# Six key pages of the attention stage summed in branch A, and two adaLN pieces and q's last transposes later, in a hybrid decoder layer on one core

## The chip, the core and the metric

The kernel runs on one core of one Trainium2 chip. A core has five engines with a queue of instructions each: TensorE (PE in the profile, its weight loads PEld), VectorE (DVE), ScalarE (ACT), GpSimd (POOL) and SyncE (SP), which issues most of the transfers and computes nothing. Transfers can be issued on SP's, ACT's or POOL's queue; 16 DMA engines carry them all. The metric is the device time of one execution in microseconds (us); lower is better.

## The reference

One layer of a decoder runs for two groups that share the weights: a prompt of 512 tokens and 8 samples of one token each, 520 columns in all, with a width of 1024.

```python
sh1, sc1, g1, sh2, sc2, g2 = ada_modulation(c, ada_w, ada_b)     # silu(c) @ ada_w + ada_b, six rows
h = rms_norm(x, norm1_g) * (1.0 + sc1) + sh1
z = h @ w_in                        # -> xr, gr, q, k, v, forget logits fl, ga, gb
xc, conv_new = causal_dwconv(xr, conv_buf, conv_w, conv_b)
hr, h_last = rg_lru(xc, h0, ...)    # recurrent branch
ya = (hr * gelu(gr)) @ w_proj_a                                  # branch A
logf = log_sigmoid(fl + b_f)
yb = attend(q, k, v, logf) @ w_proj_b                            # branch B
x = x + g1 * ((sigmoid(ga) * ya + sigmoid(gb) * yb) @ w_o)
h2 = rms_norm(x, norm2_g) * (1.0 + sc2) + sh2
gu, up = split(h2 @ w_ffn_in, 2)
x = x + g2 * ((silu(gu) * up) @ w_ffn_out)                       # then a last RMSNorm
```

The prompt's `attend` is causal attention in blocks, with 16 heads of width 64. Each of the samples attends to 1024 past tokens, which lie in a cache as 8 pages of 128 tokens; a page table says which:

```python
k_all = concatenate([cache_k[page_table], k]); v_all = concatenate([cache_v[page_table], v])
s = einsum(q, k_all) * scale + Fk[query] - Fk[key]               # Fk: cumulative log forget
out = einsum(softmax(s), v_all)
```

So there are 8 x 8 = 64 key pages and as many value pages, each 128 tokens x 1024 numbers, 512 KB.

## The kernel before, in words

**Units.** Everything is held transposed, 128 rows of the width to a tile with all 520 columns. A weight matrix is taken in *units* of 128 output columns. A unit is one product: for each of two halves of the columns, 8 blocks of the inner width times 3 passes (high and low parts of weights and activations), 24 matmuls a half. `begin` (line numbers are those of the profile) opens each unit: it calls `tick` for units 0 to 41, loads weights ahead (`load_chunks`, line 186, on SP's queue, two raw buffers `wraw`), splits them into a high and a low part (`split_upto`: ACT writes `whi`, line 210, DVE writes `wlo`, line 211; three buffers each), and flushes stores. The matmuls of a unit are line 245, and the profile names them by what they write: `xr`, `gr`, `ga`, `gb`, `k`, `v`, `pa`, `pb`, `fig`, `fiu`, `fo`.

**Order.** q comes first (q6 and q7 are units 0 and 1). Then the recurrent branch in four pairs i = 0, 2, 4, 6: `conv` (product xr, then the convolution on DVE, line 893, and a split into `xch`, `xcl`), `gelu` (product gr), `gate_a` and `gate_b` (products ga, gb), `lru_gates` (small products), `lru_exp`, `lru_root`, `lru_scan`, `lru_mul`, `lru_g` (which splits `g`, line 279). For i = 0 the units are 2 to 7, for i = 2 units 8 to 15, for i = 4 units 16 to 23, for i = 6 units 24 to 31. Unit 32 is k0; units 33 to 39 and 41 are branch A (`branch_a`, product pa, eight of them), with v0 as unit 40. `decay_rows(0)` after k0 prepares the masks of two heads on POOL (lines 1113 and 1115).

Then the attention steps i = 0 to 7 follow, one for two heads each: product k(i+1), with `v_tokens` in its middle, `turn` (transposes of the probabilities to `ptt`, split into `ph` and `pl`, line 1160), product v(i+1), with `turn` and the first `scores` in its middle, `values` (matmuls `po`), the rest of `scores`. `scores` leaves half the scaling of the probabilities to POOL (line 1146). After them come the output product of branch B (pb), the merge (wo), and the FFN (fig, fiu, fo), which takes more than a third of the time.

**Key pages.** The samples' scores are computed on DVE. For each page `page_load` reads its number from the table and issues the load (line 622), into one of seven buffers `pg`; `key_sums` multiplies it by the sample's q, copied to all partitions (`qb`; line 667, or line 663 for half pages), and sums over each head (line 668 or 664) into `S`. `key_pages` takes the next entries of a list of 64, of which the first 16 are pairs of half pages of samples 0 and 1. `tick` calls both: sums for entries that were loaded two ticks ago (one tick for the first units), then `KEYS[n]` new loads for unit n, and in the attention steps the four calls of `at(i, 0..3)` with `KEYS_AT`. When both samples of a pair r are complete, a chain of softmax steps (`past_softmax`: lines 704, 706, then `lgt`, `lgm`, `lgs` on TensorE) starts, one step every second tick. `VALUES` and `VALUES_AT` say at which ticks a pair of value pages is multiplied on TensorE (`pv`, line 751); the next pair is loaded as soon as one is used. Before, POOL's queue takes key and value loads up to the count in `LAST_LRU`, that is units 0 to 31, and SP's queue all later ones. The buffers `pg` are shared by key pages, value pages, `qb` of samples 2 to 7, and the adaLN weights.

**adaLN pieces.** Shift and scale of the first norm are made at the start (`first_mod`). The next two rows (gate1 and shift2) are `which` = 1: eight pieces of 128 rows of `ada_w`; `ada_load` loads two buffers `araw` on SP's queue (line 296), `ada_piece` runs 8 matmuls (line 308) into one PSUM bank, `ada_copy` copies it out, `ada_end` transposes it and adds the bias on DVE (line 324). PSUM has eight banks, and every half product takes one.

**q's last rows.** `q_done` copies the samples' columns of a finished q tile, stores it, and transposes the samples' columns on TensorE (line 796, `qt`); with the fourth tile `q_samples` scales and stores them to `qtd`, from where `qb` is loaded.

The order of instructions on each queue follows the program, with a planner that may let an instruction pass one that it holds not to be ready; `tc.issue_after` and `in_place` bind single ones.

Of the kernel before, what the change touches and what calls it, by code (L numbers as in the profile page):

```python
# [64 lines left out]
def kernel(ctx, tc, xT, par, gates, b_f, cst, cse, own, cache_k, cache_v, cache_lf, pt,  # L65
# [3 lines left out]
    pe, act, dve, pool, sp = nc.tensor, nc.scalar, nc.vector, nc.gpsimd, nc.sync  # L69
# [90 lines left out]
    state = {"n": 0, "dma": 0, "split": 0, "load": 22, "lead": 11, "due": 0, "age": 1}  # L160
# [8 lines left out]
    def flush():  # L169
        while stores:  # L170
# [1 line left out]

    later = {}

    KEYS = dict(zip(range(42), (2, 2, 2, 0, 3, 3, 3, 2, 1, 1, 1, 1, 2, 2, 2, 1, 0, 1, 0, 1, 2, 2, 2, 2, 0, 1, 1, 1, 2, 2, 1, 2,
                                1, 1, 1, 1, 1, 1, 1, 1, 0, 0)))
    VALUES = (19, 21, 23, 25, 27, 29, 31, 35, 37, 39)
    LAST_LRU = 32

    def load_chunks(upto):  # L180
        while state["dma"] < len(chunks) and state["dma"] <= upto:
# [76 lines left out]
    def product(name, a, evac, mid=None):  # L258
        n = begin()
        for j in range(2):  # L260
            b = bank(f"{name}_{j}")
            half_product(n, j, a, b)
            evac(j, b[:, :HALF])
            if j == 0 and mid is not None:
                mid()
        run_later(n)
# [23 lines left out]
    def ada_load(which, kq):  # L290
        if kq >= KT:
            return
        for g2 in range(2):
            raw = pgp.tile([128, 2, 512], F32, name="araw", tag="pg")
            c0 = which * 2048 + g2 * 1024
            sp.dma_start(raw, ada_w[kq * 128:kq * 128 + 128, c0:c0 + 1024].rearrange("p (g c) -> p g c", g=2))
            ada_raw.setdefault((which, kq), []).append(raw)

    def ada_piece(which, kq):
        if kq == 0:  # L300
            ada_acc[which] = bank(f"ada{which}")
        acc = ada_acc[which]
        if (which, kq) not in ada_raw:
            ada_load(which, kq)
        for g2, raw in enumerate(ada_raw.pop((which, kq))):
            for gg in range(2):
                g = 2 * g2 + gg
                pe.matmul(acc[32 * g:32 * g + 32, :], lhsT=silc[:, kq], rhs=raw[:, gg],
                          start=kq == 0, stop=kq == KT - 1, tile_position=(0, 32 * g))

    def ada_copy(which):
        sb = slot("adas", 512)
        act.copy(sb, ada_acc[which])
        ada_acc[which] = sb
# [80 lines left out]
    def past_sums(b):  # L395
        lk, after = lks[b]
        sf = bank(f"suf{b}")
        pe.matmul(sf, lhsT=cs[:, C_TRI:C_TRI + 128], rhs=lk, start=True, stop=False)
        pe.matmul(sf, lhsT=ones, rhs=after, start=False, stop=True)
        t = slot("suf", 512)  # L400
        act.copy(t, sf)
        suf.append(t)


    h = []
# [68 lines left out]
    for f in range(KT):  # L474
        t = slot("sq1")
# [14 lines left out]
    for f in range(KT):  # L490
        t = slot("xn")
# [48 lines left out]
    qtd = drp.tile([NS, D], F32, name="qtd")  # L540
# [73 lines left out]
    def page_load(cache, s, j, pg=None, c0=0, c1=D):  # L614
        if pg is None:
            pg = pgp.tile([128, D], F32, name="pg", tag="pg")
        n = s * NPAGE + j
        eng = pool if state["n"] <= LAST_LRU else sp
        done = loads[eng]
        with tc.issue_after(done[-4].ins) if len(done) >= 4 else nullcontext():  # L620
            r = eng.value_load(ptb[0:1, n:n + 1], min_val=0, max_val=NPOOL - 1)
        done.append(eng.dma_start(pg, cache[bass.ds(r, 1), :, c0:c1].rearrange("a p c -> (a p) c")))  # L622
        return pg
# [19 lines left out]
    def key_page(s, j, half=None):  # L643
        if half is not None:
            return key_halves(s, j, half)
        if j == 0:
            t = pgp.tile([128, D], F32, name="qb", tag="pg")
            (pool if state["n"] <= LAST_LRU else sp).dma_start(t, qtd[s:s + 1, :].partition_broadcast(128))
            qb[0] = t
        pg = page_load(cache_k, s, j)  # L650
        pend.append([0, s, j, pg, qb[0], None])
# [141 lines left out]
    def q_done(i, t):  # L793
        pool.tensor_copy(q8[:, NS * i:NS * i + NS], t[:, NP:])
        sp.dma_start(qd[i], t)
        pe.transpose(qtp[i // 4][:, 128 * (i % 4):128 * (i % 4) + 128], t[:, NP:], ident)
        if i % 4 == 3:
            q_samples(i // 4)
# [30 lines left out]
    for i in range(KT):  # L829
        if i % 4 == 0:  # L830
            qtp.append(bank(f"qt{i}", NS))
        if i < 6:
            t = qpart[i]
            for j, (t0, t1) in enumerate(HALVES):
                b = bank(f"q{i}_{j}")
                for k in range(4):
                    q_matmuls(1, i, j, k, b)
                dve.tensor_tensor(t[:, t0:t1], b[:, :HALF], t[:, t0:t1], ALU.add)
        else:
            t = slot("q")  # L840
            product(f"q{i}", h, to(t, act.copy))
        if ready:
            q_done(*ready.pop())
        ready.append((i, t))
        if i == 3:
            split_upto(0)
        if i == 3:
            for n in range(KT):
                gate_load(n)
        if i >= 4:  # L850
            for n in (2 * i - 8, 2 * i - 7):
                gate_split(n)
        if i == 4:
            past_load()
            split_upto(1)
            close = forget_logits()
        if i == 6:
            close()
            with tc.issue_after(state["last"].ins), tc.issue_after(state["act"].ins):
                decay()  # L860
                past_conv()
            past_turn(0)
        if i == 7:
            past_turn(1)
        if i >= 2:
            ada_piece(1, i - 2)
            ada_load(1, i - 1)
        if i == 3:
            q_done(*ready.pop())
        if i == 5:  # L870
            tick(2, 0)
    q_last = ready.pop()
# [5 lines left out]
    g = [None] * KT  # L878
    lru = {}

    def conv(i, mid=None):
        xr, xc = slot("xr"), slot("xc")

        def evac(j, b):
            t0, t1 = HALVES[j]
            act.copy(xr[:, t0:t1], b)
            act.activation(xc[:, t0:t1], b, AF.Identity, scale=cw[3], bias=prm[:, i, P_CB:P_CB + 1])

        cw = [prm[:, i, P_CW + n:P_CW + n + 1] for n in range(4)]
        product(f"xr{i}", h, evac, mid)  # L890
        for n in range(3):
            d = 3 - n
            dve.scalar_tensor_tensor(xc[:, d:NP], xr[:, :NP - d], cw[n], xc[:, d:NP], ALU.mult, ALU.add)
        dve.tensor_tensor(xc[:, NP:], xc[:, NP:], conv_past[:, i], ALU.add)
        act.copy(conv_tail[:, i], xr[:, NP - 3:])
        lru[i] = {"xc": xc}

        def close():
            lru[i].update(xs=split("xc", xc), gw=gws.pop(i))

        defer(0, close)
# [55 lines left out]
    def both(fn, i):  # L957
        fn(i)
        fn(i + 1)
# [17 lines left out]
        store(tAd[i], tA[i])  # L977

    for i in range(0, KT, 2):
        conv(i, None if i else lambda: q_done(*q_last))  # L980
        if i == 0:
            ada_piece(1, 6)
            ada_load(1, 7)
        else:
            both(lru_root, i - 2)
            gelu(i - 2)
            lru_scan(i - 2)
        conv(i + 1)
        if i == 0:
            ada_piece(1, 7)  # L990
            ada_copy(1)
        else:
            gelu(i - 1)
            lru_scan(i - 1)
            both(lru_mul, i - 2)
            both(lru_g, i - 2)
        if i < 6:
            gate_a(i)
            lru_gates(i)
            if i == 0:  # L1000
                ada_end(1)
            gate_a(i + 1)
            lru_gates(i + 1)
            gate_b(i)
            if i == 0:
                past_sums(0)
            gate_b(i + 1)
            if i == 0:
                past_sums(1)
            both(lru_exp, i)  # L1010
            if i == 2:
                log_forget()
            if i == 4:
                sum_forget()
        else:
            lru_gates(i)
            gate_a(i)
            lru_gates(i + 1)
            gate_a(i + 1)
            both(lru_exp, i)  # L1020
            gelu(i)
            both(lru_root, i)
            gelu(i + 1)
            both(lru_scan, i)
            both(lru_mul, i)
            both(lru_g, i)
# [233 lines left out]
            q_load(1)  # L1260
    g = None
    state.update(load=14, lead=8)
    KEYS_AT = [(0, 2, 0, 0)] * 3 + [(0, 0, 0, 0)] * 5
    VALUES_AT = [(1, 1, 0, 1)] * 6 + [(1, 1, 0, 1), (1, 0, 0, 0)]

    def at(i, part):
        tick(KEYS_AT[i][part], VALUES_AT[i][part])
        flush()

    for i in range(KT):  # L1270
# [313 lines left out]
```

## Time and profile before

| | us |
|---|---|
| three runs, median (lowest to highest) | 1081.26 (1080.08 to 1083.93) |
| the profiled execution | 1082.19 |
| its span, first to last instruction | 1080.5 |
| TensorE busy | 1029.1 |
| VectorE busy | 663.9 |
| ScalarE busy | 494.4 |
| GpSimd busy | 192.2 |

The profile is of one execution; times in it count from the span's start. In its rows L245 is a line of the kernel, `out<-in` names the tiles, 128x1024 is partitions by elements, x48 a count; what follows `<-` in brackets is what ended an engine's idle time before the row. "Granted clock" is the share of TensorE's full clock that it was given. `whi`, `wlo` and the like are named without their numbers, so which unit a split belongs to is counted from the order.

### The profile page before, as it was taken

How to read it: one execution, taken by the hardware profiler on the slowest of the kernel's cores; microseconds unless marked ns; L12 is line 12 of the kernel's file. 1: busy time of each engine (PE TensorE's matmuls, PEld its weight loads, DVE VectorE, ACT ScalarE, POOL GpSimd, SP SyncE). 2: the span in 40 equal slices, each digit the busy share in tenths (PEclk: the TensorE clock that was granted, in tenths of full speed). 3: DMA queues.
4: the chain of work that ended last, by engine and by line, in shares of the span. 5: the costliest groups of instructions: out<-in, count | busy, mean ns of one | idle time of the engine just before them, and what ended most of it. 6: DMA issues, size and time to landing. Idle time of an engine off the chain costs nothing.

```text
span 1080.5 us, 21007 instructions
## 1 busy us (share of the span) xinstructions
PE 1029.1 (95%) x8210; PEld 951.7 (88%) x8210; DVE 663.9 (61%) x1166; ACT 494.4 (46%) x976; POOL 192.2 (18%) x328
## 2 busy tenths in 40 slices
PE   4999899999999988899999999999999999999994
PEld 2887699999999977688888979999999999999994
DVE  5437899989989766766656546843343333433363
ACT  4423565856772455577784224533212233113251
POOL 0224320112132223433420003300000000000013
PEclk9999899999999998899999999999999999999998
DMA  9799976878879979877874764124224233233112
GB/s 329 270 316 325 302 253 175 260 258 295 253 257 292 300 251 267 263 227 239 246 247 165 262 241 108 41 78 117 79 82 115 79 88 109 79 94 103 59 59 80
DMA packets 165285, 206.95 MB, mean 192 GB/s; under 512 B 9778, under 2 KB 126018, under 8 KB 165122
## 3 DMA queue, kind: packets, MB, share of 16 engines
q1 hardware_dynamic: 150626, 160.39, 47.8%
q0 software_dynamic: 10880, 38.80, 10.6%
q10 hardware_dynamic: 3680, 6.42, 1.6%
q8 instruction: 64, 1.05, 0.4%
q14 instruction: 35, 0.29, 0.1%
HBM read 192.49 MB, written 13.09 MB: 190 GB/s over the span
## 4 chain that ended last, share of the span: by engine, by line
PE 74%; DVE 10%; DMA 7%; ACT 4%; issue 3%; POOL 1%; SPq 0%; POOLq 0%; DVEq 0%; ACTq 0%
PE fig L245 11%; PE fiu L245 11%; PE fo L245 10%; PE v L245 4%; PE pb L245 4%; PE pa L245 4%; PE k L245 4%; PE gb L245 3%; DMA wraw<-in_w_in_dram 3%; PE pv L751 3%; PE wo L245 3%; PE xr L245 2%; PE gr L245 2%; DMA araw<-in_ada_w_dram 2%; PE qp L467 2%
## 5 line engine op out<-in xcount | busy, mean ns | idle before, releaser
L211 DVE TENSOR_TENSOR wlo<-wraw,whi 128x1024 fp32r<-128x1024 f32 (+1 forms) x131 | 160.6, 1227 | 161.0 <-ACT whi L210 160.7
L210 ACT CAST whi<-wraw 128x1024 fp32r<-128x1024 f32 (+1 forms) x131 | 136.6, 1043 | 229.3 <-PE fo L245 74.5
L245 PE MATMUL fiu<-h2h,wlo 128*128 128x260 f32 x320 | 90.5, 283 | 0.0
L245 PE MATMUL fig<-h2h,wlo 128*128 128x260 f32 x320 | 90.5, 283 | 0.0
L245 PE MATMUL fig<-h2l,whi 128*128 128x260 f32 x320 | 90.1, 282 | 0.0
L245 PE MATMUL fiu<-h2l,whi 128*128 128x260 f32 x320 | 90.0, 281 | 0.0
L245 PE MATMUL fig<-h2h,whi 128*128 128x260 f32 x320 | 90.0, 281 | 0.0
L245 PE MATMUL fiu<-h2h,whi 128*128 128x260 f32 x320 | 90.0, 281 | 0.0
L337 POOL TENSOR_TENSOR ss<-ss,sq 128x260 f32<-128x260 f32 x18 | 13.5, 752 | 418.9 <-ACT sq L336 418.4
L245 PE MATMUL fo<-ach,whi 128*128 128x260 f32 x292 | 82.6, 283 | 0.0
L245 PE MATMUL fo<-ach,wlo 128*128 128x260 f32 x292 | 82.5, 283 | 0.0
L245 PE MATMUL fo<-acl,whi 128*128 128x260 f32 x292 | 82.3, 282 | 0.0
L667 DVE TENSOR_TENSOR pg<-pg,qb 128x1024 f32<-128x1024 f32 x48 | 58.1, 1222 | 4.4 <-DMA pg<-in_cache_k_dram 4.3
L245 PEld LDWEIGHTS fiu<-h2l,whi 128*128 128x128 f32 x320 | 60.3, 188 | 0.0
L245 PEld LDWEIGHTS fig<-h2l,whi 128*128 128x128 f32 x320 | 60.3, 188 | 0.0
L245 PEld LDWEIGHTS fiu<-h2h,whi 128*128 128x128 f32 x320 | 60.3, 188 | 0.0
L245 PEld LDWEIGHTS fig<-h2h,whi 128*128 128x128 f32 x320 | 60.2, 188 | 0.0
L245 PEld LDWEIGHTS fig<-h2h,wlo 128*128 128x128 f32 x320 | 60.1, 188 | 0.0
L245 PEld LDWEIGHTS fiu<-h2h,wlo 128*128 128x128 f32 x320 | 60.1, 188 | 0.0
L668 DVE TENSOR_REDUCE S<-pg 128x16 f32<-128x1024 f32 x48 | 57.4, 1206 | 0.2
L622 POOL DMA_DIRECT2D pg<-in_cache_k_dram x66 | 35.2, 533 | 111.4 <-DVE S L668 59.8
L245 PEld LDWEIGHTS fo<-ach,whi 128*128 128x128 f32 x292 | 54.9, 188 | 0.0
(388 smaller groups left out, 3454.4 us busy)
## 6 DMA issues: line engine op xcount, KB each, us to landing
araw<-in_ada_w_dram SPq DMA_DIRECT2D x48, 512.0 KB, 6.8
pg<-in_cache_v_dram SPq DMA_DIRECT2D x48, 512.0 KB, 5.0
wraw<-in_w_fi_dram SPq DMA_DIRECT2D x44, 512.0 KB, 3.9
wraw<-in_w_in_dram SPq DMA_DIRECT2D x34, 512.0 KB, 7.8
pg<-in_cache_k_dram POOLq DMA_DIRECT2D x34, 512.0 KB, 5.1
wraw<-in_w_in_dram SPq DMA_DIRECT2D x11, 1024.0 KB, 9.2
pg<-in_cache_k_dram POOLq DMA_DIRECT2D x32, 256.0 KB, 6.1
pg<-in_cache_v_dram POOLq DMA_DIRECT2D x16, 512.0 KB, 5.3
```

The costliest lines, as they stand in the source:

```text
L210: state["act"] = act.copy(hi[:, :k1 - k0], src)
L211: state["last"] = dve.tensor_tensor(lo[:, :k1 - k0], src, hi[:, :k1 - k0].bitcast(F32), ALU.subtract)
L245: state["mm"] = pe.matmul(out[:, :HALF], lhsT=wt[k], rhs=at, start=k == 0 and m == 0, stop=k == nk - 1 and m == 2)
L337: eng.tensor_tensor(acc[:, t0:t1], acc[:, t0:t1], q_, ALU.add)
L467: state["mm"] = pe.matmul(b[:, :HALF], lhsT=wt, rhs=at[:, t0:t1], start=k == 0 and m == 0, stop=k == 3 and m == 2)
L622: done.append(eng.dma_start(pg, cache[bass.ds(r, 1), :, c0:c1].rearrange("a p c -> (a p) c")))
L667: dve.tensor_tensor(pg, pg, q, ALU.mult)
L668: dve.tensor_reduce(S[r // 2][:, c:c + H], pg.rearrange("p (h d) -> p h d", d=DH), AX.X, ALU.add)
L751: pe.matmul(pv[0][32 * gq:32 * gq + 32, :], lhsT=pw[r][:, c:c + 32], rhs=pgs[gq // 2][:, 512 * hf:512 * hf + 512], start=j == 0, stop=j == ...
```

## The change

Four parts:

1. The six key pages loaded in attention steps 0 to 2 (two in each, `KEYS_AT`) go to earlier units: unit 24 loads one more, units 33, 35, 37 and 39 load two and no longer one, and unit 40 loads one. Nothing is loaded in the attention steps any more. All pages from unit 24 on move up in the list.
2. `LAST_LRU` = 32 becomes `LAST_POOL` = 40: page loads of units 32 to 39 (key pages, value pages and `qb`) are issued on POOL's queue, as those before them.
3. adaLN pieces 6 and 7 move from the first recurrent pair (after units 2 and 3) to the second (after units 8 and 10), with their copy and `ada_end` (from behind unit 4's gates to behind unit 12's). The load of piece 6 is issued after unit 7, that of piece 7 after piece 6.
4. `q_done` of q7 no longer runs between the halves of xr0's product, but behind it.

```diff
-    KEYS = dict(zip(range(42), (2, 2, 2, 0, 3, 3, 3, 2, 1, 1, 1, 1, 2, 2, 2, 1, 0, 1, 0, 1, 2, 2, 2, 2, 0, 1, 1, 1, 2, 2, 1, 2,
-                                1, 1, 1, 1, 1, 1, 1, 1, 0, 0)))
+    KEYS = dict(zip(range(42), (2, 2, 2, 0, 3, 3, 3, 2, 1, 1, 1, 1, 2, 2, 2, 1, 0, 1, 0, 1, 2, 2, 2, 2, 1, 1, 1, 1, 2, 2, 1, 2,
+                                1, 2, 1, 2, 1, 2, 1, 2, 1, 0)))
     VALUES = (19, 21, 23, 25, 27, 29, 31, 35, 37, 39)
-    LAST_LRU = 32
+    LAST_POOL = 40
...
-        eng = pool if state["n"] <= LAST_LRU else sp
+        eng = pool if state["n"] <= LAST_POOL else sp
...
-            (pool if state["n"] <= LAST_LRU else sp).dma_start(t, qtd[s:s + 1, :].partition_broadcast(128))
+            (pool if state["n"] <= LAST_POOL else sp).dma_start(t, qtd[s:s + 1, :].partition_broadcast(128))
...
         if i >= 2:
             ada_piece(1, i - 2)
-            ada_load(1, i - 1)
+            if i < 7:
+                ada_load(1, i - 1)
...
     for i in range(0, KT, 2):
-        conv(i, None if i else lambda: q_done(*q_last))
+        conv(i)
         if i == 0:
-            ada_piece(1, 6)
-            ada_load(1, 7)
+            q_done(*q_last)
         else:
+            if i == 2:
+                ada_piece(1, 6)
+                ada_load(1, 7)
             both(lru_root, i - 2)
             gelu(i - 2)
             lru_scan(i - 2)
         conv(i + 1)
-        if i == 0:
-            ada_piece(1, 7)
-            ada_copy(1)
-        else:
+        if i:
+            if i == 2:
+                ada_piece(1, 7)
+                ada_copy(1)
             gelu(i - 1)
...
-            if i == 0:
+            if i == 2:
                 ada_end(1)
...
             if i == 0:
                 past_sums(1)
+                ada_load(1, 6)
...
-    KEYS_AT = [(0, 2, 0, 0)] * 3 + [(0, 0, 0, 0)] * 5
     VALUES_AT = [(1, 1, 0, 1)] * 6 + [(1, 1, 0, 1), (1, 0, 0, 0)]
 
     def at(i, part):
-        tick(KEYS_AT[i][part], VALUES_AT[i][part])
+        tick(0, VALUES_AT[i][part])
         flush()
```

More of the change, by code (lines that the diff above doesn't have):

```diff
@@ L879, with conv @@
     lru = {}
-    def conv(i, mid=None):
+    def conv(i):
         xr, xc = slot("xr"), slot("xc")
@@ L889, in conv @@
         cw = [prm[:, i, P_CW + n:P_CW + n + 1] for n in range(4)]
-        product(f"xr{i}", h, evac, mid)
+        product(f"xr{i}", h, evac)
         for n in range(3):
```

## The prediction

> **What bounds the kernel now.** I read the page first, then the busy time by stretch, then the chain of work that ended last, the waits, and the instructions in order of time. The page says that TensorE has little room:
>
> ```profile
> span 1080.5 us, 21007 instructions
> ## 1 busy us (share of the span) xinstructions
> PE 1029.1 (95%) x8210; PEld 951.7 (88%) x8210; DVE 663.9 (61%) x1166; ACT 494.4 (46%) x976; POOL 192.2 (18%) x328
> ```
>
> So 1080.5 - 1029.1 = 51.4 us are idle, and a change can win only where TensorE idles or runs slowly. The stretches show where. Columns: stretch, its length, then busy us (and instructions) of PE, weight load, DVE, ACT and POOL, the granted clock, the DMA share and GB/s. The first two rows are evenly cut; from 315.30 on I cut at the starts of products: rows 3 to 5 are units 33 to 41 (branch A's output product with v0 in it), rows 6 to 12 the attention steps i = 0 to 6.
>
> ```profile
> 162.00:189.00 27.00, 25.62 (x207) 24.73 (x205) 27.00 (x39) 14.73 (x26) 2.11 (x4) 1.00 0.67 175
> 297.00:324.00 27.00, 26.22 (x217) 25.02 (x216) 23.07 (x33) 20.54 (x34) 10.02 (x11) 1.00 0.76 257
> 315.30:335.60 20.30, 19.52 (x158) 17.85 (x156) 20.15 (x29) 5.84 (x11) 7.57 (x12) 1.00 0.80 258
> 335.60:355.20 19.60, 19.60 (x161) 17.66 (x160) 19.04 (x28) 6.79 (x8) 0.00 (x0) 1.00 1.01 312
> 355.20:375.40 20.20, 20.20 (x167) 20.01 (x164) 15.12 (x32) 10.66 (x28) 3.82 (x5) 1.00 1.03 321
> 375.40:403.40 28.00, 25.12 (x179) 21.16 (x178) 17.34 (x33) 14.09 (x34) 8.43 (x16) 0.94 0.77 250
> 403.40:433.50 30.10, 26.32 (x181) 21.91 (x177) 20.44 (x43) 17.97 (x46) 10.84 (x17) 0.89 0.84 245
> 433.50:464.60 31.10, 26.65 (x183) 22.06 (x179) 21.78 (x48) 17.78 (x44) 11.10 (x17) 0.89 0.85 255
> 464.60:488.40 23.80, 23.77 (x181) 19.71 (x180) 15.74 (x38) 17.85 (x47) 10.58 (x17) 1.00 0.85 244
> 488.40:511.60 23.20, 23.20 (x183) 19.81 (x179) 15.03 (x41) 16.27 (x42) 9.96 (x17) 1.00 0.78 251
> 511.60:535.60 24.00, 23.73 (x183) 19.83 (x179) 15.76 (x36) 18.69 (x47) 10.59 (x17) 1.00 0.81 242
> 535.60:558.50 22.90, 22.90 (x179) 19.36 (x176) 14.81 (x38) 17.32 (x44) 9.09 (x15) 1.00 0.69 231
> ```
>
> Steps 0 to 2 take 28.0, 30.1 and 31.1 us, steps 3 to 6 take 23.8, 23.2, 24.0 and 22.9 us for the same 179 to 183 matmuls. Steps 0 to 2 are those that load two key pages each; in them the clock falls to 0.94, 0.89 and 0.89. The chain (columns: start, us, what ran) and TensorE's waits (total us, times, the longest) say what happens there.
>
> ```profile
> 393.65 4.66 PE v L245 x24
> ...
> 479.53 3.14 PE v L245 x24
> ```
>
> ```profile
> PE v L245 <- DVE pl L1160: 6.7, 3, 2.3
> PE ada L308 <- DMA araw<-in_ada_w_dram: 4.8, 2, 4.4
> PE adaf L416 <- DMA araw<-in_ada_w_dram: 1.8, 3, 0.7
> PE qt L796 <- ACT q L271: 1.5, 1, 1.5
> ...
> PE ga L245 <- DVE pw L721: 1.1, 1, 1.1
> ```
>
> Three times the second half of v waits about 2.2 us for pl, the low part of the turned probabilities; its 24 matmuls then take 4.66 us (step 0) where step 3 takes 3.14. On VectorE the key pages stand ahead of pl; this is step 0, in order of time:
>
> ```profile
> 388.32 1.22 DVE L667 TENSOR_TENSOR pg<-pg,qb 128x1024 f32<-128x1024 f32 x1
> ...
> 391.78 1.21 DVE L667 TENSOR_TENSOR pg<-pg,qb 128x1024 f32<-128x1024 f32 x1
> 392.91 1.28 DVE L1160 TENSOR_TENSOR pl<-ptt,ph 128x512 fp32r<-128x512 f32 x2
> ```
>
> **The change part by part.** *Attention steps 0 to 2.* Six key pages leave (`KEYS_AT` goes): six loads on SP, six multiplies and six reduces on VectorE. If the three steps then run like steps 3 to 6, whose mean is (23.8 + 23.2 + 24.0 + 22.9) / 4 = 23.5 us, they shrink from 89.2 to 70.4: **-18.8**. The least that can come back is TensorE's idle time in them, 2.88 + 3.78 + 4.45 = 11.1 us; the most is three steps like the quickest, 89.2 - 68.7 = 20.5. I take 18.8: steps 3 to 6 run the same code with the same value pages, and their clock is 1.00. The last softmax chain (r = 3) starts in step 0 instead of step 3; it moves from one side of this sum to the other. Value index 24, the first that needs it, still comes in step 4. The one page that is pending at step 0, and the chain's first reduces, fall into the 28.00 - 17.34 = 10.7 us that VectorE idles in that step.
>
> *Units 33 to 40 (branch A).* Five pages come in: one more at units 33, 35, 37 and 39, and the last at unit 40. A page costs one multiply and one reduce on VectorE and a load of 512 KB, 0.524 MB:
>
> ```profile
> L667 DVE TENSOR_TENSOR pg<-pg,qb 128x1024 f32<-128x1024 f32 x48 | 58.1, 1222 | 4.4 <-DMA pg<-in_cache_k_dram 4.3
> L668 DVE TENSOR_REDUCE S<-pg 128x16 f32<-128x1024 f32 x48 | 57.4, 1206 | 0.2
> ```
>
> ```profile
> pg<-in_cache_k_dram POOLq DMA_DIRECT2D x34, 512.0 KB, 5.1
> ...
> pg<-in_cache_k_dram SPq DMA_DIRECT2D x14, 512.0 KB, 5.1
> ```
>
> VectorE: 5 x 2.43 = 12.1 us. What hides it is the lead of the weight splits over TensorE. VectorE works through rows 3 and 4 nearly without idle time, but it gains on TensorE: at the end of the stage the split of unit 42 (first row, in order of time) is done at 363.30 + 1.23 = 364.5 for k1, which starts at 375.51 (second row, the chain), 11.0 us later.
>
> ```profile
> 363.30 1.23 DVE L211 TENSOR_TENSOR wlo<-wraw,whi 128x1024 fp32r<-128x1024 f32 x1 [1.59 <-ACT whi L210]
> ```
>
> ```profile
> 375.51 2.89 PE k L245 x24
> ```
>
> A page is summed two units after its load, so three of the five (7.3 us) stand ahead of unit 42's split and leave it 3.7 us; the other two meet VectorE's idle time, 20.20 - 15.12 = 5.1 us in row 5 and more in step 0. VectorE alone costs nothing here. DMA does not have that room: its share is 1.01 and 1.03 from 335.6 on. Five pages are 2.62 MB, at (312 + 321) / 2 = 317 GB/s 8.3 us, and only row 3 has room, 0.20 x 20.3 = 4.1 us. I take the rest, **+4.2**, as time that the stage grows by. Its ends are 0 (late data use up the 3.7 us of lead, or spill into step 0, where the share is 0.77) and 12.1 (none of VectorE's added work is hidden); the value lies nearer to 0 because the 11.0 us of lead is a row of this very stage.
>
> `LAST_POOL` = 40 moves the key loads of units 32 to 39, now 12, three pairs of value loads and one qb from SP's queue to POOL's. On POOL, k0's small product, the mask adds for heads 0 and 1 and the scaling of p for step 0 stand among them. POOL is busy 0.00 us in row 4, and both queues land a page in 5.1 us, so I cost the move at nothing; the cover is that POOL has so little else to do there. SP loses waits that stood ahead of weight loads; but those wait for the split of an earlier chunk anyway, so I count no gain.
>
> *Unit 24's page, and r = 2's chain.* One page more at unit 24 moves all later ones up one place. Its 2.43 us come before the 27.00 - 23.07 = 3.93 us that VectorE idles in 297 to 324: nothing. But the sums of r = 2 are complete one unit sooner, at unit 31, and the first step of its chain (L704 and L706) then goes ahead of g's split, for which branch A's first product waits:
>
> ```profile
> 318.87 0.69 DVE L704 TENSOR_TENSOR S<-S,suf 128x128 f32<-128x128 f32 x2
> 319.47 1.22 DVE L211 TENSOR_TENSOR wlo<-wraw,whi 128x1024 fp32r<-128x1024 f32 x1
> 320.61 0.61 DVE L706 TENSOR_REDUCE mk<-S 128x32 f32<-128x256 f32 x1
> ```
>
> 0.69 + 0.61 = **+1.3** (0, or 1.3 + 2.4 = 3.7 if the page is late as well).
>
> *The adaLN pieces and q's last rows.* Piece 6 loads after unit 7 and runs after unit 8, piece 7 after unit 10; `ada_end` goes from unit 4 to unit 12. TensorE's waits of 4.4 us (ada) and 1.5 us (qt) go. VectorE limits what that is worth: it is busy 27.00 of 27.00 us in 162 to 189, so TensorE comes out earlier only by what VectorE gains. That is the idle time ahead of this page, whose load shared the DMA with adaLN's:
>
> ```profile
> 114.30 1.23 DVE L663 TENSOR_TENSOR pg<-pg,qb 128x1024 f32<-128x1024 f32 x1 [2.67 <-DMA araw<-in_ada_w_dram]
> ```
>
> Against -2.7 stands a PSUM bank that is held from unit 4 to unit 12, where ga's second half already waits for one (1.1 us): together **-1.6**. The ends are -6.3 (both waits on TensorE, 4.8 + 1.5) and +2.8 (nothing gained, and at unit 8 one adaLN wait like the 4.4 now, less the 1.6 that I count). Piece 6's load asks for two of the seven page buffers on SP's queue; the weights behind it wait for splits anyway, and the key pages of the next units come later by two buffers, which is the +2.8 end. The pieces' own matmuls only move. q's last transposes come half a unit later, and with them the store that key loads two units on read; VectorE's queue hides that.
>
> **Sum.** -18.8 + 4.2 + 1.3 - 1.6 = **-14.9 us**; what follows the attention steps starts earlier by it and keeps it. The profiled execution took 1082.19 us (1.7 around its span of 1080.5), the median of three runs is 1081.26, 0.9 lower. I count from the median: 1081.3 - 14.9 = 1066.4.
>
> **The rivals.** (a) *Only the idle time comes back* in steps 0 to 2 and the slow matmuls stay: -11.1 for -18.8, -7.2 in all, **1074.1**. For it: no single wait of v is over 2.3 us. Against it: 3.14 us and clock 1.00 in step 3. The Trainium skill ("TensorE: Matmul & The Clock Gate", "Why this matters for your kernels") names idle gaps beyond about 3 us as what throttles. By that rule gaps of 2.3 us don't, and taking them away would not bring the clock back: 1074.1. The trace, with 0.89 in just these steps, does not agree.
>
> (b) *Branch A hides nothing*: 12.1 for 4.2, -7.0 in all, **1074.3**. For it: VectorE is busy 20.15 of 20.30 and 19.04 of 19.60 us in rows 3 and 4. Against it: 11.0 us of lead at unit 42.
>
> (c) *Slower: POOL's queue.* A page load on POOL waits for a free buffer, and what stands behind it waits too:
>
> ```profile
> POOL pg L622 <- DVE S L668: 75.9, 24, 9.2
> ```
>
> 75.9 / 24 = 3.2 us each. If each of the eight units 33 to 40 loses 3.2 us by it, branch A costs 25.3 and not 4.2: +6.2, **1087.5**. It ends slower from (18.8 + 1.6 - 1.3) / 8 = 2.4 us a unit on. For it: SP, where these loads are now, has no arithmetic behind them. Against it: the 24 waits stand there now, and TensorE's waits name no POOL load. The Trainium skill ("DMA: Bandwidth & Descriptors", "SWDGE vs HWDGE vs iDMA") speaks for it: GpSimd writes the descriptors of its own loads into SBUF, where VectorE can lock it out, and loads from SP are immune. The equal 5.1 us of the two queues do not show that.
>
> (d) *The change doesn't do what it says*: steps 0 to 2 keep their length, bound by the value pages: -1.6 + 4.2 + 1.3 = +3.9, **1085.2**. Steps 3 to 6, with the same value pages, speak against it.
>
> **How the numbers follow.** Forecast 0.70 (its own range 1060 to 1072), (a) 0.10, (b) 0.10, (c) 0.05, (d) 0.03, better than 1058 0.02. The range 1058 to 1076 takes in (a) and (b); its low end is the good ends of the attention and branch A terms with the early part as costed, -20.5 - 1.6 = -22.1, 1059, and a little. About 0.3%, 3.2 us, is what a measurement of this kernel tells from no change. The first three cases and the last are faster; (c) and (d) are slower, less 0.01 of them that ends near zero, as do 0.02 of (a) and (b) together: faster 0.90, same 0.03, slower 0.07.
>
> **What would show it.** Right: steps 0 to 2 near 23.5 us at clock 1.00 with no wait of v for pl; branch A longer by some 4 us with the DMA share near 1.0; TensorE 1 to 3 us earlier at unit 14; 47 whole-page key loads on POOL and one on SP. Wrong: v still over 4 us, TensorE waiting for weight splits at units 35 to 42, POOL's masks or scaled p late, or adaLN matmuls waiting near unit 8.

## The result, and the profile after

| | before | after |
|---|---|---|
| median of the runs taken together (lowest to highest) | 1081.5 (1080.08 to 1083.93) | 1068.68 (1066.89 to 1071.45) |
| the same, taken once more on another occasion | 1080.07 (1078.67 to 1081.89) | 1067.93 (1067.42 to 1068.45) |
| the profiled execution | 1082.19 | 1067.71 |
| its span | 1080.5 | 1066.1 |

The ratio after / before is 0.9881 with a 95% interval of [0.9852, 0.9911], the second time 0.9888 [0.9873, 0.9903]: some 12.5 us faster. Forecast were 1066.4 us and -14.9 us. Line numbers after the change are up to 4 higher in the attention code (v's `pl` is L1164, the scores are L1136 and L1137).

The page of the kernel after, its first rows:

```profile
span 1066.1 us, 21006 instructions
## 1 busy us (share of the span) xinstructions
PE 1021.3 (96%) x8210; PEld 948.1 (89%) x8210; DVE 664.0 (62%) x1166; ACT 494.2 (46%) x976; POOL 202.2 (19%) x348
```

The work is the same (8210 matmuls; VectorE 664.0 us against 663.9). TensorE idles 44.8 us instead of 51.4, and it is busy 7.8 us less for the same matmuls, because they ran at a higher granted clock (0.987 over the span against 0.979). Cut by stretch, as the prediction cut it (three rows of units 33 to 41, then the attention steps 0 to 4):

```profile
314.20:335.40 21.20, 18.23 (x132) 16.47 (x131) 21.06 (x29) 6.03 (x12) 10.97 (x18) 0.92 0.76 218
335.40:357.00 21.60, 21.60 (x180) 20.61 (x178) 21.45 (x31) 5.93 (x8) 4.22 (x8) 1.00 1.06 382
357.00:377.90 20.90, 20.90 (x169) 19.86 (x169) 19.20 (x34) 10.46 (x27) 4.66 (x8) 1.00 1.09 337
377.90:401.60 23.70, 23.42 (x182) 19.71 (x181) 18.86 (x41) 15.68 (x38) 8.88 (x16) 1.00 0.98 289
401.60:425.70 24.10, 23.94 (x182) 19.82 (x178) 15.66 (x39) 17.42 (x45) 11.58 (x17) 1.00 0.92 282
425.70:449.00 23.30, 23.30 (x185) 19.91 (x181) 15.60 (x41) 17.93 (x45) 11.18 (x17) 1.00 0.93 245
449.00:471.80 22.80, 22.80 (x178) 19.33 (x177) 14.64 (x34) 17.23 (x45) 10.53 (x17) 1.00 0.86 260
```

Steps 0 to 2 are 23.7, 24.1 and 23.3 us long where they were 28.0, 30.1 and 31.1, and their clock is 1.00 where it was 0.94, 0.89 and 0.89. Units 33 to 41 lose clock in the first row only (0.92); the other two are full, although the DMA share is now 1.06 and 1.09. TensorE's waits of the kernel after (total us, times, the longest):

```profile
PE gate L915 <- DVE xcl L279: 2.8, 1, 2.8
PE ada L308 <- DMA araw<-in_ada_w_dram: 2.3, 2, 1.8
PE adaf L416 <- DMA araw<-in_ada_w_dram: 2.2, 3, 0.7
PE lgm L718 <- DVE dg L713: 1.8, 1, 1.8
...
PE gate L915 <- ACT xch L278: 1.3, 1, 1.3
PE pa L245 <- DVE gl L279: 1.1, 2, 0.6
```

Of v's waiting for pl (6.7 us) one wait of 0.28 us is left, further down that list. New are the waits of the first pair's gate matmuls at 115 and 119 us, and of lgm, a step of a softmax chain, for dg. In step 0 VectorE goes from v's low part straight into pl, without a key page between:

```profile
390.44 0.42 DVE L1102 TENSOR_TENSOR v<-vt,v 128x256 fp32r<-128x256 f32 x1
390.78 3.07 DVE L1164 TENSOR_TENSOR pl<-ptt,ph 128x512 fp32r<-128x512 f32 x5
```

Where the time went, by the starts of the same matmuls in the two profiled executions: unit 14 starts 1.1 us sooner, and from there to the first pa both take 124.8 us; from the first pa to step 0's k it takes 63.8 us instead of 60.1 (+3.7); steps 0 to 2 take 71.05 us instead of 89.23 (-18.2); steps 3 to 6 are 1.2 shorter together, step 3 by 1.0, for which the chain of r = 3, now in step 0, is the likely reason; and from gb6 to the end it takes 524.3 us instead of 522.0 (+2.3), of which 1.6 lie behind the last product. The sum is -14.5, the difference of the spans 14.4.

### The profile page after: what moved, and what is told of

Same layout as the page of the kernel before. It is cut to its first block, busy times and chain, and to the rows that moved or that the text cites. A ratio compares the mean times of both kernels' runs of the same rounds, so it can differ in the third digit from the quotient of the medians.

```text
span 1066.1 us, 21006 instructions
## 1 busy us (share of the span) xinstructions
PE 1021.3 (96%) x8210; PEld 948.1 (89%) x8210; DVE 664.0 (62%) x1166; ACT 494.2 (46%) x976; POOL 202.2 (19%) x348
## 4 chain that ended last, share of the span: by engine, by line
PE 76%; DVE 9%; issue 4%; DMA 4%; ACT 4%; POOL 2%; POOLq 1%; SPq 0%; ACTq 0%; DVEq 0%
PE fiu L245 11%; PE fig L245 11%; PE fo L245 9%; PE pb L245 4%; PE k L245 4%; PE v L245 4%; PE pa L245 3%; PE gr L245 3%; PE gb L245 3%; PE ga L245 3%; PE xr L245 3%; PE wo L245 3%; PE pv L751 3%; DMA wraw<-in_w_in_dram 2%; PE qp L467 2%
## 5 line engine op out<-in xcount | busy, mean ns | idle before, releaser
L622 POOL DMA_DIRECT2D pg<-in_cache_k_dram x79 | 42.1, 533 | 115.8 <-DVE S L668 61.1
L245 PEld LDWEIGHTS fig<-h2h,wlo 128*128 128x128 f32 x320 | 60.1, 188 | 0.0
L245 PEld LDWEIGHTS fiu<-h2h,wlo 128*128 128x128 f32 x320 | 60.1, 188 | 0.0
L245 PEld LDWEIGHTS fo<-ach,wlo 128*128 128x128 f32 x292 | 55.1, 189 | 0.0
```

The lines of the kernel that those rows point to most:

```text
L245: state["mm"] = pe.matmul(out[:, :HALF], lhsT=wt[k], rhs=at, start=k == 0 and m == 0, stop=k == nk - 1 and m == 2)
```

## Experiments

My theory for the attention steps: VectorE works its queue in order, and the two instructions per key page that stand ahead of pl make v late. Its rivals: the pages' loads did it (DMA share, or the queue that issues them). For branch A, whose growth I had put down to DMA, the traces asked for another theory: the chain of r = 2 runs a unit sooner and meets a VectorE that has no idle time. All numbers, side by side; "early" is the start of unit 14 (gb2), the others are lengths from the first pa to step 0's k and of steps 0 to 2, all from each kernel's one profile; those of keys alone and of page 24 at unit 41 are of the slowest of their runs (1073.2 and 1078.63 us). Each ratio goes against runs of the kernel before on the same chip, whose medians were 1080.1 to 1081.5:

| kernel | median us | ratio to before [95%] | early | pa to k | steps 0-2 |
|---|---|---|---|---|---|
| before | 1080.2 | 1 | 190.5 | 60.1 | 89.2 |
| after | 1068.68 | 0.9881 [0.9852, 0.9911] | 189.3 | 63.8 | 71.1 |
| after, again (a2) | 1067.93 | 0.9888 [0.9873, 0.9903] | 191.3 | 62.3 | 71.1 |
| keys alone (e1) | 1071.29 | 0.9905 [0.9886, 0.9924] | 193.8 | 62.3 | 70.9 |
| adaLN and q alone (e2) | 1082.88 | 1.0025 [1.0012, 1.0037] | 188.5 | 60.1 | 89.8 |
| before, small sums (e7) | 1068.41 | 0.9894 [0.9876, 0.9911] | 188.4 | 60.1 | 73.9 |
| after, five loads gone (e6b) | 1067.55 | 0.9880 [0.9865, 0.9895] | 191.3 | 62.3 | 70.7 |
| after, pages on SP (e3) | 1069.56 | 0.9901 [0.9886, 0.9916] | 190.0 | 63.9 | 72.6 |
| after, chain later (c2) | 1063.63 | 0.9863 [0.9838, 0.9888] | 188.6 | 60.8 | 71.1 |
| the same, again | 1066.59 | 0.9870 [0.9853, 0.9886] | 191.3 | 61.1 | 71.4 |
| after, page 24 at unit 41 (e4) | 1074.04 | 0.9936 [0.9913, 0.9958] | 192.4 | 68.2 | 72.7 |
| after, adaLN in third pair (e5) | 1075.36 | 0.9949 [0.9931, 0.9968] | 191.4 | 63.7 | 70.9 |
| after, adaLN a unit later (c3) | 1071.88 | 0.9920 [0.9906, 0.9934] | 192.4 | 63.8 | 70.9 |
| that with two chains later (c5) | 1070.23 | 0.9910 [0.9897, 0.9924] | 191.9 | 60.8 | 71.9 |

**The two parts of the change, each alone.** The keys' part:

```diff
-    KEYS = ...  0, 1, 1, 1, 2, 2, 1, 2,  1, 1, 1, 1, 1, 1, 1, 1, 0, 0)))
+    KEYS = ...  1, 1, 1, 1, 2, 2, 1, 2,  1, 2, 1, 2, 1, 2, 1, 2, 1, 0)))
-    LAST_LRU = 32
+    LAST_POOL = 40
-        tick(KEYS_AT[i][part], VALUES_AT[i][part])
+        tick(0, VALUES_AT[i][part])
```

> Only parts 1 and 2 of the change (key pages and the queue); adaLN pieces and q's transposes stand as before. If the parts add up, as my sum has them, steps 0 to 2 give 18 us and branch A costs 3.7, 14.5 us under the kernel before, and the adaLN wait of 4.4 us on TensorE is back. Rival: the early part is needed for the pages to fit, and branch A costs more than 6 us without it.

The part with adaLN and q is the rest of the change, with the four places above as before:

> Only parts 3 and 4 (adaLN pieces 6 and 7, q's transposes); key pages and their queues as before. My sum: 1.6 us under the kernel before; the changed kernel's trace: 1.1 us at unit 14. Rival (the waits that go on TensorE count in full): 6.3 us.

The keys alone bring steps 0 to 2 to 70.9 us and the time to 0.9905. The adaLN and q part alone is no gain: 1.0025 [1.0012, 1.0037]. By the medians the two do not add up to the whole, which is some 3 us below the keys alone; the intervals overlap, so it is not settled whether the early part helps beside the keys. The early part differs from profile to profile by more than the forecast term: unit 14 started at 188.4, 190.5 and 193.8 us in the three profiles with the old order, and at 188.5 to 192.4 us in the eight that have the new one as the change made it. What the early edits are worth within the whole is therefore not settled; alone they gain nothing.

**Steps 0 to 2: VectorE's work or the loads?** In the kernel before, the six pages stay where they are and are loaded as before, but VectorE's two instructions are cut to 64 columns:

```diff
...
+                if half == -1:
+                    dve.tensor_tensor(pg[:, :64], pg[:, :64], q[:, :64], ALU.mult)
+                    dve.tensor_reduce(S[...], pg[:, :64].rearrange("p (h d) -> p h d", d=4), AX.X, ALU.add)
...
```

> The kernel before, with the six key pages of attention steps 0 to 2 still loaded where they were, but multiplied and summed over their first 64 columns alone (the other 960 columns' scores of these pages are left out). Theory (VectorE's order: the two whole-page instructions ahead of pl make v wait): the waits of v for pl of 2.1 to 2.3 us go, steps 0 to 2 fall from 89.2 us to 71 to 74, the clock in them is 1.00, time 1062 to 1066 us. Rival (the pages' loads, by DMA share or by the queue that issues them, lengthen these steps): they stay at 85 us or more, time 1075 to 1081.

The stretches of steps 0 to 2 in this kernel:

```profile
373.30:397.10 23.80, 23.43 (x181) 19.60 (x179) 13.79 (x35) 14.32 (x34) 9.30 (x16) 1.00 0.81 264
397.10:420.90 23.80, 23.54 (x180) 19.56 (x176) 14.46 (x35) 15.70 (x41) 9.48 (x17) 1.00 0.96 292
420.90:447.20 26.30, 24.11 (x182) 19.82 (x179) 20.17 (x53) 19.74 (x49) 12.37 (x17) 1.00 0.94 283
```

With all six loads in place the steps take 73.9 us at clock 1.00: 15.3 of the 18.2 us come from VectorE's instructions alone, and of v's waits for pl one of 0.37 us is left. Step 2 keeps 26.3 us; its transposes `ptt` wait for VectorE (1.2 us for `ksB`) and for ACT (0.7 us for `ph`). The median, 1068.41, is 2.4 us above what I expected.

**Branch A: the loads.** The kernel after, where five of its pages (those that the last units got) are not loaded and the page before them is summed again:

```diff
-        pg = page_load(cache_k, s, j)
+        if N_KEYS - len(keys_todo) - 1 in AGAIN:
+            pg = last_pg[0]
+        else:
+            pg = last_pg[0] = page_load(cache_k, s, j)
```

> The kernel after, but the five pages that branch A got from the attention steps are not loaded: the page loaded last is multiplied and summed again in their place (their own scores are left out; VectorE's work is the same to the instruction). My recorded term (2.62 MB more in branch A make it 4.2 us longer): the stretch from the first pa to step 0's k falls from 63.8 us to about 60, time 1064 to 1066. Theory now (the growth comes from the softmax chain of r = 2, which runs one unit earlier and finds VectorE without idle time): the stretch stays at 63 to 64.5, lgm still waits 1.8 us for dg, time 1067.5 to 1070.

From the first pa to step 0's k, without the five loads:

```profile
316.10:378.40 62.30, 59.34 (x480) 55.55 (x478) 61.68 (x92) 22.43 (x46) 17.62 (x30) 1.00 0.95 293
```

and with them, in the repeat of the kernel after (a2):

```profile
316.10:378.40 62.30, 59.34 (x480) 55.54 (x478) 60.65 (x91) 21.68 (x44) 20.14 (x33) 1.00 0.96 309
```

The two agree to the hundredth in TensorE's busy time, and both profiles show the same wait of 1.83 us. The five loads cost this stretch no time; my term of 4.2 us for them was wrong. Where they are left out, two weight loads and a value page that otherwise come later are issued within the stretch, so it moves only 1.0 MB less (293 against 309 GB/s over 62.3 us) and the share stays at 0.95. A share near 1.0 did not say here that the stretch is bound by the DMA engines.

**Branch A: the chain of r = 2.** VectorE's instructions ahead of the wait, in the kernel after (`st` and `dg` are the chain's):

```profile
321.92 2.36 DVE L667 TENSOR_TENSOR pg<-pg,qb 128x1024 f32<-128x1024 f32 x2
324.19 2.34 DVE L668 TENSOR_REDUCE S<-pg 128x16 f32<-128x1024 f32 x2
326.56 0.28 DVE L711 TENSOR_REDUCE st<-lgt 32x1 f32<-32x128 f32 x1
...
328.58 1.20 DVE L667 TENSOR_TENSOR pg<-pg,qb 128x1024 f32<-128x1024 f32 x1
329.71 0.53 DVE L713 TENSOR_SCALAR dg<-cs,st 32x256 f32<-32x256 f32 x1
```

and TensorE at that place:

```profile
327.49 1.07 PE L751 MATMUL pv<-pg,pw 128*32 128x512 f32 x8
330.39 0.67 PE L718 MATMUL lgm<-dg,cs 32*128 32x256 f32 x2 [1.83 <-DVE dg L713]
```

Two page products with their sums stand ahead of `st`, and a weight split, the evacuation of pa and one more product between `st` and `dg`. TensorE asks for dg 14.4 us after the first pa; before, it asked 19.7 us after it, one unit later. VectorE got there 16.7 us after the first pa before and 15.6 after: it is busy 37.86 of the 38 us around it (307 to 345) and, with its work in this order, can't come sooner. If that is the cause, asking one unit later mends it:

```diff
...
         store(mtd[32 * r:32 * r + 32, 0:1], st)
+        if r == 2:
+            hold(r, -1)
         yield False
...
         act.activation(t[:, :256], L, AF.Exp)
+        if r == 2:
+            hold(r, 1)
         yield False
```

`hold` sets the chain's tick counter: lgm comes after three ticks and not two, the step behind it after one.

> The kernel after, with the second step of the softmax chain of r = 2 (lgm) one unit later and the step behind it one unit sooner; nothing is left out. Theory (the chain's place made branch A longer): lgm's wait of 1.83 us and the slow 24 pa matmuls behind it (4.45 us against 2.98) go, pa to k takes 60 to 61 us, time 1065 to 1066.5. Rival (VectorE has no idle time from 307 to 345 us, so that it sets the end of the stretch wherever the chain stands): another wait for VectorE of about 2 us shows up in the stretch, it stays at 62.5 to 64, time 1068 to 1070.

> The kernel after once more, as the measure of the next three on the same chip: 1066.5 to 1071 us by its first runs, pa to k 62.3 to 63.8 us (62.3 where the 24 matmuls behind lgm's wait keep their clock, as they did in two of the five profiles that have this wait).

> The kernel after with the second step of the softmax chain of r = 2 one unit later, once more. If its 1063.63 us is the chain's place, it stays 2 to 5 us below the kernel after on the same chip, 1063 to 1066 us, with pa to k at 60 to 61 us; if it was the spread of the runs, the two medians agree within 1.5 us.

TensorE at lgm with the chain later, first profile:

```profile
333.50 0.28 PE L245 MATMUL pa<-gl,whi 128*128 128x260 f32 x1
333.71 0.69 PE L725 MATMUL lgm<-dg,cs 32*128 32x256 f32 x2
334.33 0.39 PE L245 MATMUL pa<-gh,whi 128*128 128x260 f32 x1
```

The wait is gone and nothing takes its place in the stretch: 60.8 and 61.1 us in its two profiles against 63.8 and 62.3 (and 60.8 in the two-chains kernel below, which has the same edit). This shows the cause of most of branch A's growth. What is left over the 60.1 of before is mainly the second wait for g's split (0.64 us, the row "2 times" above). On the whole time the first comparison gave 1063.63 us, the second 1066.59 beside 1067.93 of the kernel after on the same chip. That is 1.3 us, which by the expectation counts as spread. The later chain has the lowest median of all kernels both times; whether it beats the change itself is not settled, for the intervals overlap.

**Unit 24's page, moved to the end.** This puts the chain of r = 2 back to its old unit by other means:

```diff
-    KEYS = ...  1, 1, 1, 1, 2, 2, 1, 2,  1, 2, 1, 2, 1, 2, 1, 2, 1, 0)))
+    KEYS = ...  0, 1, 1, 1, 2, 2, 1, 2,  1, 2, 1, 2, 1, 2, 1, 2, 1, 1)))
```

> The changed kernel, but unit 24's added page goes to unit 41, so that the softmax chain of samples 4 and 5 starts at unit 32 again, as before. If that chain, one unit early on a VectorE queue without lead, makes the 1.83 us wait of lgm and the slow matmuls behind it, both go, and branch A shrinks from 63.8 us to about 60.5; time 3 us under the changed kernel. Rival (the DMA share sets branch A's length): branch A stays at 63 us or more, and step 0 grows by a page's 2.4 us.

The wait of lgm is gone here too, but another appears, and the kernel is slower than after (1074.04). TensorE, then ACT, at that place:

```profile
371.98 0.58 PE L1136 MATMUL sc<-ksB,qqB 128*128 128x256 f32 x1 [3.39 <-ACT row L731]
```

```profile
370.80 1.04 ACT L210 CAST whi<-wraw 128x1024 fp32r<-128x1024 f32 x1 [7.82 <-DMA wraw<-in_w_in_dram]
371.75 0.17 ACT L731 COPY row<-lgs 1x32 f32<-1x32 f32 x1
```

The scores wait 3.39 us for `row`, the chain's last copy on ACT. That copy takes 0.17 us, but in ACT's queue it stands behind a weight cast, which waits for its weights. Their load was issued at 356.69 us and landed at 370.70, 14.0 us later, while the page loads that POOL issued from 353 to 368 us took 6.6 to 8.7 us. A slow weight load alone is not the difference: the kernel with the later chain has one of 15.4 us in this stretch and no such wait. The order on ACT is: in the kernel before, where the chain has the same unit, `row` ran at 361.41 us, ahead of the next cast at 362.21; here it stands behind the cast that waits. The wait and the slow matmuls behind it are read from one profile, of the slowest run; how much of the median's 5 to 6 us they make is open.

**POOL's queue.** The pages of units 33 to 40 back on SP's queue:

```diff
-    LAST_POOL = 40
+    LAST_POOL = 32
```

> The kernel after, with the pages of the units behind the 32nd issued on SP's queue, as before the change, and not on POOL's; nothing is left out. If the queue is of no account (VectorE's order alone makes the gain): pa to k at 62 to 64.5 us, steps 0 to 2 at 70.5 to 72, time 1066.5 to 1071. If the pages, which wait for a free buffer, hold up the weights queued behind them on SP: a wait for wraw or for what a late cast holds up (row, as in the run with a page at unit 41) of 2 to 6 us in branch A or in step 0, time 1072 to 1077. If the recorded rival on POOL's queue had a part, attention steps 1 and 2 come out shorter than 23.2 us: no trace so far asks for that.

Its stretches from pa to k, and of step 0:

```profile
314.80:378.70 63.90, 60.82 (x478) 57.03 (x477) 59.22 (x90) 22.77 (x47) 13.56 (x16) 0.97 0.85 277
378.70:404.00 25.30, 24.83 (x182) 19.88 (x180) 21.70 (x42) 14.08 (x36) 11.29 (x16) 1.00 0.91 256
```

Branch A is as long as in the first profile of the kernel after, step 0 is 1.7 us longer (25.3), the median 1.6 us above that of the repeat on the same chip. The intervals overlap: the queue is of small account in these stages, and POOL's is, if anything, the better one. At the kernel's end it is the other way round (see the part on the prediction).

**The early part: what sets its pace.** In the kernel after, piece 6 waits 1.79 us for its weights at 152 us. Three kernels take that wait away: the pieces in the third pair (`if i == 4` for `if i == 2`, the load after the second pair), the pieces one unit later on TensorE, and that with lgm of r = 0 (and of r = 2) later as well:

```diff
...
-            if i == 2:
-                ada_piece(1, 6)
-                ada_load(1, 7)
             both(lru_root, i - 2)
             gelu(i - 2)
+            if i == 2:
+                ada_piece(1, 6)
+                ada_load(1, 7)
             lru_scan(i - 2)
...
```

> The changed kernel, but adaLN pieces 6 and 7 run in the third recurrent pair (after units 16 and 18), with the load of piece 6 after unit 15. If the wait for piece 6's data at unit 8 (1.79 us and slow matmuls, 2.57 us for the 8) is what eats the early gain, unit 14 comes 3 us earlier than in the changed kernel, and the end too. Rival (VectorE, full in 135 to 190 us, sets the time of unit 14 anyway): within 1 us of the changed kernel.

> The kernel after, with the adaLN pieces 6 and 7 one unit later on PE (behind gr instead of behind xr); nothing is left out, and the loads' issue places are the same. Theory (from 112 to 188 us VectorE has no idle time and sets the pace): the wait of 1.8 us for araw and the slow matmuls go, but a wait for pw of 1 to 4 us comes before ga near 182 us; unit 14 (gb2) starts at 188.5 to 190.5 as before, time 1067 to 1071. Rival (the wait for araw sets the pace of this part): unit 14 starts at 185.5 to 187, time 1064 to 1066.

> The same with the adaLN pieces 6 and 7 one unit later on PE and the second step of the chain of r = 0 one unit later too; nothing is left out. Theory (the wait for pw at 182 us comes from the bank that lgm holds while VectorE is behind): neither the wait for araw nor the one for pw is there, unit 14 starts 2 to 4 us sooner than in the kernel after (185.5 to 187.5), time 1060 to 1063 us. Rival (VectorE, without idle time from 112 to 188 us, sets the start of unit 14 whatever PE does): another wait for VectorE of 1.5 us or more stands between 155 and 190 us, unit 14 starts at 188.5 to 191, time 1063.5 to 1067.

All three have higher medians than the kernel after; the interval of the third pair is clear of both of its intervals, that of c3 of one of them, that of c5 of neither. With the pieces one unit later (c3), TensorE and VectorE near 182 us:

```profile
182.56 0.58 PE L245 MATMUL ga<-hh,whi 128*128 128x260 f32 x1 [3.96 <-DVE pw L721]
```

```profile
182.46 0.08 DVE L721 MEMSET pw<- 128x24 f32 x1
```

and with both chains later (c5), TensorE and ACT:

```profile
183.09 0.39 PE L245 MATMUL ga<-hh,whi 128*128 128x260 f32 x1 [3.62 <-ACT tA L982]
```

```profile
179.77 0.62 ACT L278 CAST gh<-ge 128x520 fp32r<-128x520 f32 x1 [1.60 <-DVE ge L955]
180.30 1.04 ACT L210 CAST whi<-wraw 128x1024 fp32r<-128x1024 f32 x1
181.35 1.28 ACT L982 ACT_TABLE_LOAD   x1
182.65 0.67 ACT L982 ACTIVATE tA<-ga 128x260 f32<-128x260 f32 x2
```

TensorE comes sooner and then waits at 182 us for VectorE: for the chain's step on VectorE that reads lgm's PSUM bank and the memset behind it (c3; 4.83 us in the third-pair kernel), or, when lgm is out of the way, for an activation that stands in ACT's queue behind a cast of VectorE's `ge` (c5). Either way ga starts at 181.8 to 183.1 us, and in the kernel after it starts at 182.06 without a wait. Why nothing helps can be read from one view of the kernel after:

```profile
112.00:182.00 70.00, 63.52 (x470) 57.76 (x470) 69.49 (x99) 37.34 (x69) 15.46 (x29) 0.95 0.86 264
307.00:345.00 38.00, 35.03 (x272) 32.48 (x271) 37.86 (x55) 14.49 (x24) 16.23 (x25) 0.96 0.86 281
```

VectorE (the third of the engines) is busy 69.49 of 70 us in the one stretch and 37.86 of 38 in the other. The wait for weights at 152 us costs nothing that these kernels could win back: without it the idle time comes back later and in one piece, and the matmuls behind it run slowly (c3's 24 ga matmuls take 5.6 us instead of 3.1). Where the rest of their loss lies is shown for one of them: in the third-pair kernel it takes 129.2 us from unit 14 to the first pa, in each of the other thirteen profiles 124.8. There the pieces run where TensorE has hardly any idle time (128.22 us busy of the 129.20), and so cost their own time; in the second pair TensorE waits for VectorE anyway. Unit 14 of c3 and c5 starts at 192.4 and 191.9 us, no later than that of some kernels with the change as made, so their loss is not located.

## Why the prediction was right, step by step

- **Steps 0 to 2, -18.8:** measured -18.2. By the starts of the matmuls the steps came to 23.6, 24.2 and 23.3 us where the forecast had 23.5 each, the longest wait of v for pl is 0.28 us, and the small-sums kernel shows VectorE's instructions as the cause.
- **Branch A, +4.2 for DMA:** wrong. It measured 0 with the loads left out. The share above 1.0 was read as a bound, but no wait of TensorE in the stage is for a load. The step that failed is "I take the rest, +4.2, as time that the stage grows by".
- **The chain of r = 2, +1.3:** the mechanism was named only in part and the size was too small. The part named, the two instructions ahead of g's split, cost 0.67 us between pa's first and third half. The larger part came one step later in the same chain: 1.83 us of waiting for dg and, in the first profile, 1.5 us of slow matmuls behind it. Together branch A grew by 2.2 to 3.7 us, forecast were 5.5; the two errors cancelled in part, which is luck.
- **Loads moved to POOL at nothing:** held within the stages, where on SP they cost no less, but not at the kernel's end. POOL's last long instruction is a DRAIN, which ends 0.8 us before the span does while the other engines wait. Counted from its issue it takes 11.22 us where it took 9.53 (before, then after; the last of the three numbers, in ns):

```profile
L1568 POOLq DRAIN  x3: 46/104/9531, 1070.2 to 1080.2; - x3
```

```profile
L1571 POOLq DRAIN  x3: 46/104/11219, 1054.0 to 1065.8; - x3
```

  From the start of the last fo matmul to the end it takes 15.64 us in the three kernels that issue 91 loads on POOL, 15.72 with 92 (e3), 16.96 with 107 (e6b), 17.20 with 110 (e4) and 17.27 to 17.28 in all eight with 111. That is 0.08 us for each load, so the 20 that moved cost 1.6 us. What the drain does in this time no trace shows. The kernel after issues 79 key loads on POOL, of which 32 are half pages, so 47 whole ones, and one on SP, as forecast:

```profile
L622 POOL DMA_DIRECT2D pg<-in_cache_k_dram x79: 527/530/548, 73.3 to 361.1; - x79
...
L622 SPq DMA_DIRECT2D pg<-in_cache_k_dram x1: 352/352/352, 363.3 to 363.3; - x1
```

- **adaLN and q, -1.6:** 1.1 us between the two profiles, the first in the step's favour; but repeats of unit 14 spread by more, and alone the part is 2.7 us slower. The idle time of 2.67 us ahead of the page is gone, as forecast. The reason given, that VectorE and not TensorE's waits limits this part, fits what the three kernels above show: 12.0 us gained at the first ga are 5.2 at gb0 and 1.1 at gb2, the first of the loss being the gate matmuls' new waits for VectorE and ACT. A wait near unit 8, named among the signs of being wrong, did come (1.79 us), and no kernel without it was faster.
- **"What follows keeps it":** 2.3 us were given back between gb6 and the end, 1.6 of them by POOL's drain, which is the step of the sum that put the moved loads at nothing. The other 0.7 is within the spread: without the end behind the last fo matmul this stretch took 506.2 to 509.9 us over the fourteen profiles.
- **Rival (a)**, that the slow matmuls stay, needs gaps of 2.3 us not to throttle; the clock of 1.00 in steps 0 to 2 refutes it. **(b)** is refuted by branch A's length, **(c)** by the pages on SP, **(d)** by steps 0 to 2.
- **The sum:** that it came within some 2.5 us owes most to its largest term. Branch A was put too long by 1.8 to 3.3 us and the end too short by 2.3, and these offset each other; that is luck as well.

## What to carry to other kernels

Work that fits an engine's idle time still costs if it stands in that engine's queue ahead of something that the bounding engine waits for; look for stretches where the engine idles *and* for what is behind the moved work in its queue. A wait in the trace is worth taking away only if no engine without idle time stands behind it: look first for a stretch where one is busy 99% of the time. When a change moves the point at which a chain of small steps starts, write down for each step when it is asked for and when its engine gets there. When loads move from one queue to another, look also at the kernel's end, where no wait of TensorE shows them: 20 loads more on POOL's queue cost 1.6 us there.

## What the hardware showed that was not expected

The same wait of 1.83 to 1.91 us for dg, at the same place in the program, was followed by slow matmuls in four profiles (the 24 behind it took 4.40 to 4.67 us: after, e3, e5, c3) and by matmuls at full speed in three (3.1 us: a2, e1, e6b). In the kernel after, then in its repeat, the stretch behind that wait; the granted clock is the third number from the end:

```profile
331.00:335.40 4.40, 4.40 (x25) 4.40 (x25) 4.40 (x7) 0.00 (x0) 1.52 (x3) 0.63 0.95 194
```

```profile
333.00:336.20 3.20, 3.20 (x28) 3.20 (x28) 3.20 (x5) 0.00 (x0) 1.49 (x3) 1.00 0.84 165
```

The slow matmuls do not begin at the end of the wait: in the kernel after the first nine behind it still take 0.28 us each, those from 332.19 to 335.22 us 0.42. The waits of 2.1 to 3.4 us between 300 and 500 us (three in before, three in e2, one in e4) all cost clock: the 24 matmuls of a product behind them took 4.7 to 5.6 us. The early part has the same toss-up with shorter waits: a wait of 1.57 us of the first ga was followed by 24 matmuls in 4.68 us (e4, 110 us), one of 1.55 us at the same place by 24 in 3.15 us (c5), and one of 1.99 us at 188 us in e1 by 24 in 3.15 us. So a gap between some 1.5 and 2 us is a toss-up here, and one kernel's profile can differ from its own repeat by 1.5 us at such a place. The Trainium skill ("TensorE: Matmul & The Clock Gate", "Why this matters for your kernels") gives idle gaps beyond about 3 us as what throttles. The runs here do not agree: waits of 1.83 to 1.91 us were enough in four of seven, and one of 1.57 us in e4.
